# A written four-chunk cycle for the gate stage, rows from chunk 26 on, and a fifth row buffer

## The chip, the core and the metric

The kernel runs on one core of one Trainium2 chip. The metric is the device time of the whole program in microseconds; smaller is better.

## What is computed

The reference is two transformer blocks over 256 tokens of width 1024. Everything that the change touches lies in the last part of the second block, an expert layer (PEER) with 16,384 experts. Cut to that part:

```python
def peer_ffn(h, w_pq, peer_keys, peer_u, peer_v):
    q = (ht @ w_pq).reshape(T, 8, 2, 128)
    sub = jnp.einsum('thpc,hpnc->thpn', q, peer_keys)
    s_top, i_top = lax.top_k(sub, 16)
    ...                                        # 16 best pairs of each head
    best_s, pos = lax.top_k(cand_s, 16)
    expert = jnp.take_along_axis(cand_i, pos, axis=-1)
    gate = jax.nn.softmax(best_s, axis=-1)     # 8 heads x 16 = 128 experts a token
    def chunk(args):
        xc, ec, gc = args
        u = jnp.take(peer_u, ec, axis=0)
        act = jax.nn.gelu(jnp.einsum('cd,ckd->ck', xc, u))
        vv = jnp.take(peer_v, ec, axis=0)
        return jnp.einsum('ck,ckd->cd', gc * act, vv)
```

`peer_u` and `peer_v` are 16,384 x 1024 in float32, 64 MiB each.

## The kernel before

The kernel computes the expert layer in two ways at once. For the last 160 tokens (`N`) it is dense: all experts' scores are computed, multiplied by a gate that is zero for experts not chosen, and the result is summed over all experts. For the first 96 tokens (`TS`) it is sparse: only the chosen experts' rows are fetched.

**The dense part, score stage.** The experts come in 128 chunks of 128. `wget_raw` hands out the next weight tile of 128x1024 float32 (0.524 MB), which SyncE loads ahead (`_dma`) into a ring of 13 buffers (`home`, with `RB` = 3; four more for a time at the start). For each chunk eight products (`u_dot`, L1599; each is two matmul records in the trace, 16 a chunk) write one PSUM bank of a ring of three (`psum`). For chunks 0 to 43 (`u_chunk`, L1609) ScalarE writes the gelu of it into `act`. From chunk `U0` = 44 on (`u_mul`), tokens whose gate is already known get their gelu into a buffer `ut` (L1617; four buffers, `UT`) and VectorE multiplies it into the gate that stands in `act` (L1620); the other tokens' gelu goes straight into `act` (L1619).

**The gates.** `topk` finds the chosen experts of a token as a pair of indices and a gate; `pick` transposes them so that `ib` and `jb` hold the two indices and the gate, in two float16 parts (`gb[0]` high, `gb[1]` low). `g_batch` makes the gates of 8 tokens for all experts: VectorE builds one-hot tiles (`onehots`: `eq` L1543, `jo` L1544, and `io` as `eq` times the high and the low gate, L1546), 16 float16 matmuls (L1555) make a 128x128 gate matrix of each token in PSUM, and that is multiplied into finished chunks of `act` by VectorE (L1564) or copied by ScalarE (L1566) into chunks yet to come. There are 20 batches, spread over chunks 44 to 125.

**The output stage.** Chunk by chunk, eight products of a `peer_v` tile with `act` add up in four PSUM banks (`acc`, L1684).

**The sparse part.** `sparse` is a generator; each step fetches one 128x1024 tile of expert rows (0.524 MB) by an indirect DMA that GpSimd issues (L1503) into one of `SB` = 4 buffers `ug`. The first 96 steps take rows of `peer_u`, and VectorE multiplies them with the tokens' vectors and sums (L1508). Then the next 96 take rows of `peer_v`, and VectorE adds them, weighted, to `sacc` (L1520). At the end TensorE sums `sacc` over pairs (`pair`, L1698), the columns go into `fT` (L1691, L1693, L1702), are transposed back (`back`, L1675), added to `xl` (L1677), normalized and stored. The copies of `acc` into `fT` on VectorE are ordered behind the last row step.

In the program text, rows start at chunk 44: `step()` after every chunk asks for 192 steps in 222 chunks. The program is ordered for each engine by a planner that simulates the time; an instruction that stands later in the text may be drawn forward on its engine where the planner sees it ready. `behind` adds an order between two instructions of one engine for the planner, without a wait on the chip. The loads of GpSimd's queue (`xl`, `slot`, rows) stand in one order, too.

Of the kernel before, what the change touches and what calls it, by code (L numbers as in the profile page):

```python
# [9 lines left out]
F32 = mybir.dt.float32  # L10
F32R = mybir.dt.float32r
BF = mybir.dt.bfloat16
FP16 = mybir.dt.float16
# [8 lines left out]
D = 1024  # L22
# [110 lines left out]
class Kernel:  # L133
# [1240 lines left out]
    def topk(self, R, K, subs):  # L1374
        nc, V, A, G = self.nc, self.nc.vector, self.nc.scalar, self.nc.gpsimd
        iota = R.iota
        self.ib, self.jb, *self.gb = [R.pool.tile([128, 256], FP16, name=n) for n in ("ib", "jb", "g1", "g2")]
        self.iota2 = R.pool.tile([128, 128, 2], FP16, name="iota2")
        V.tensor_copy(self.iota2, iota[:, :, None].to_broadcast([128, 128, 2]))
        it16 = K.tile([128, 16, 16], FP16, name="it16")  # L1380
# [67 lines left out]
    def pick(self, K, tt, prev):  # L1448
        nc, V, A = self.nc, self.nc.vector, self.nc.scalar
        ps = self.bank(self.ptk, "tk")  # L1450
        for i, a in enumerate(self.picked[tt]):
            self.behind(nc.tensor.transpose(ps[:, 128 * i:128 * i + 128], a.rearrange("p h k -> p (h k)"), self.eye),
                        prev)
        t0 = slice(tt * 128, tt * 128 + 128)
        for d, i in ((self.ib, 1), (self.jb, 2)):
            A.activation(d[:, t0], ps[:, 128 * i:128 * i + 128], AF.Copy)
        g = K.tile([128, 128], F32, name="gres", bufs=2)
        V.tensor_scalar(g, ps[:, 0:128], GSCALE, None, op0=OP.mult)
        V.tensor_copy(self.gb[0][:, t0], g)
        V.tensor_tensor(self.gb[1][:, t0], g, self.gb[0][:, t0], OP.subtract)  # L1460


    TG = ((0, 64), (64, 32))
    TS = 96
    SB = 4

    def rows_init(self, SP):
        nc, V = self.nc, self.nc.vector
# [29 lines left out]
    def sparse(self):  # L1498
# [6 lines left out]
        slots = [(g, s) for g, (t0, n) in enumerate(self.TG) for s in range(t0, t0 + n)]  # L1505
        for g, s in slots:
            t = fetch(self.io["u_rows"], s)
            V.scalar_tensor_tensor(t, t, 1.0, self.hrow[g], op0=OP.mult, op1=OP.mult, accum_out=self.sdot[:, s:s + 1])  # L1508
            yield
        A.activation(self.sw, self.sdot, AF.Gelu_apprx_tanh)  # L1510
        V.scalar_tensor_tensor(self.sw, self.sw, GSCALE, self.slot[:, 1], op0=OP.mult, op1=OP.mult)
# [18 lines left out]
    SP = ("VVVVVG", "VVVVVG")  # L1530
    OB = (2, 2)
    U0 = 44
    SC = 222
    U1 = 126
    UT = 4

    def onehots(self, O, t0):
        V = self.nc.vector
        jo, eq = [O.tile([128, 4, 128, 2], FP16, name=n, bufs=b) for n, b in (("jo", self.OB[0]), ("eq", 1))]
        io = O.tile([128, 2, 4, 128, 2], FP16, name="io", bufs=self.OB[1])  # L1540
        bc = lambda a: a[:, t0:t0 + 8].rearrange("p (b t) -> p b t", t=2)[:, :, None, :].to_broadcast([128, 4, 128, 2])
        iob = self.iota2[:, None].to_broadcast([128, 4, 128, 2])
        V.tensor_tensor(eq, iob, bc(self.ib), OP.is_equal)  # L1543
        V.tensor_tensor(jo, iob, bc(self.jb), OP.is_equal)  # L1544
        for q in range(2):
            V.tensor_tensor(io[:, q], eq, bc(self.gb[q]), OP.mult)  # L1546
        return jo, io

    def g_batch(self, O, pg, act, t0, i):
        nc, V, A = self.nc, self.nc.vector, self.nc.scalar  # L1550
        ps = self.bank(pg, "g", 2)
        jo, io = self.onehots(O, t0)
        for t in range(8):
            for q in range(2):
                nc.tensor.matmul(ps[:, t // 4, 128 * (t % 4):128 * (t % 4) + 128], jo[:, t // 2, :, t % 2],  # L1555
                                 io[:, q, t // 2, :, t % 2], start=q == 0, stop=q == 1)
        pv = ps.rearrange("p b (t i) -> p i (b t)", t=4)
        for k in range(2):
            m = self.U0 if k == 0 else 128 - self.U0
            o = self.U0 * k  # L1560
            n = min(max(i - o, 0), m)
            w = act[k][:, :, t0 - self.TS:t0 - self.TS + 8]
            if n:
                V.tensor_tensor(w[:, 0:n], w[:, 0:n], pv[:, o:o + n], OP.mult)  # L1564
            if n < m:
                A.activation(w[:, n:m], pv[:, o + n:o + m], AF.Copy)  # L1566

    def peer(self):
        nc, V, A, G, tc = self.nc, self.nc.vector, self.nc.scalar, self.nc.gpsimd, self.tc
# [17 lines left out]
        with ExitStack() as st:  # L1587
# [18 lines left out]
            def u_chunk(i):  # L1606
                ps = self.psum()
                m = u_dot(ps[:, 0:N])
                A.activation(at(i), ps[:, 0:N], AF.Gelu_apprx_tanh)  # L1609
                return m  # L1610

            def u_mul(i, n, U):
                ps = self.psum()
                u_dot(ps[:, 0:N])
                w = at(i)
                t = U.tile([128, N], F32, name="ut")
                A.activation(t[:, 0:n], ps[:, 0:n], AF.Gelu_apprx_tanh)  # L1617
                if n < N:
                    A.activation(w[:, n:], ps[:, n:N], AF.Gelu_apprx_tanh)  # L1619
                V.tensor_tensor(w[:, 0:n], w[:, 0:n], t[:, 0:n], OP.mult)  # L1620
            with tc.tile_pool(name="route", bufs=1) as K:
                R = type("R", (), dict(iota=iota, pool=PT))
                with self.ps_pool("prt") as self.prt:
                    subs = self.route(R, K, h)
                with self.ps_pool("ptk") as self.ptk:
                    self.topk(R, K, subs)
                    self.depth = 10 + self.RB
                    for i in range(self.U0):
                        m = u_chunk(i)
                        if i == self.U0 - 4:  # L1630
                            for tt in range(2):
                                self.pick(K, tt, m)
# [2 lines left out]
            A1 = st.enter_context(tc.tile_pool(name="act1", bufs=1))  # L1635
            act.append(A1.tile([128, 128 - self.U0, N], F32, name="act1"))
            U = st.enter_context(tc.tile_pool(name="ut", bufs=self.UT))
            sparse, done = self.sparse(), [0, 0]

            def step():  # L1640
                done[0] += 1
                while done[1] * self.SC < done[0] * 2 * TS:
                    next(sparse, None)
                    done[1] += 1
            with tc.tile_pool(name="oh", bufs=2) as O, self.ps_pool("pg", 2) as pg:
                i, nb = self.U0, N // 8
                for b in range(nb):
                    self.g_batch(O, pg, act, TS + 8 * b, i)
                    while i < 128 and (i - self.U0) * nb < (b + 1) * (self.U1 - self.U0):
                        u_mul(i, 8 * b + 8, U)  # L1650
                        step()
                        i += 1
                while i < 128:
                    u_mul(i, N, U)
                    step()
                    i += 1
            pa = st.enter_context(self.ps_pool("pa"))
            acc = [self.bank(pa, f"acc{i}") for i in range(4)]
            x = self.bt.tile([128, 2, 1024], F32, name="xl", tag="bighi")
# [21 lines left out]
            for i in range(128):  # L1681
                w = self.wget_raw()
                for d in range(8):
                    nc.tensor.matmul(part(d), w[:, 128 * d:128 * d + 128], at(i),  # L1684
                                     start=i == 0 and d % 2 == 0, stop=i == 127, skip_group_check=True)
                step()
            for _ in sparse:
                pass
            for d in range(8):
# [80 lines left out]
```

## Time and profile before

| | |
|---|---|
| median of 3 runs | 1314.06 us (1309.58 to 1322.44) |
| profiled execution | 1311.89 us, span 1309.8 us |
| granted TensorE clock, mean | 0.969 |
| TensorE matmul busy | 1238.3 us (95%) |
| VectorE busy | 909.0 us (69%) |
| ScalarE busy | 447.7 us (34%) |
| GpSimd busy | 445.3 us (34%) |
| moved from and to HBM | 356.22 MB read, 2.12 MB written |

Busy time is a share of the whole span; a stage's limit is read from the stage. Of 0.524 MB loads there are 128 of `peer_u`, 128 of `peer_v` and 192 tiles of rows. The score stage runs from 675.6 to 978.7 us, the output stage from 978.9 to 1284.3.

### The profile page before, as it was taken

What the parts mean: (1) busy time and instruction counts of PE and PEld (TensorE: products, weight loads), DVE (VectorE), ACT (ScalarE), POOL (GpSimd) and SP (SyncE); (2) the same over time, 40 slices, a digit from 0 to 9 for tenths busy, and PEclk for the clock granted to TensorE, in tenths of its full rate; (3) what the DMA queues carried; (4) which work ended last, traced back from release to release, by engine and by line L of the source; (5) the groups of instructions that cost most, each with busy time, mean ns of one, the idle gap of its engine ahead of it and who ended that gap; (6) DMA issues with size and microseconds to landing.
All of it is one profiled execution on the core that took longest, in us unless ns stands there. A gap on an engine that the chain in (4) does not pass through costs nothing.

```text
span 1309.8 us, 22554 instructions
## 1 busy us (share of the span) xinstructions
PE 1238.3 (95%) x8649; PEld 1158.9 (88%) x8650; DVE 909.0 (69%) x1810; ACT 447.7 (34%) x895; POOL 445.3 (34%) x400
## 2 busy tenths in 40 slices
PE   6799989999999999998999999999999999999995
PEld 5688869988979997996899999999999999888884
DVE  8996765889668897468789766777764445454455
ACT  5337655666557755645532112221110000000001
POOL 6931021555105755003300432223233333333332
PEclk9978899999999998998999999999999999999996
DMA  6322346889826655346677999999999999999993
GB/s 204 100 87 72 134 164 215 316 301 333 256 91 236 215 168 168 126 143 216 245 273 244 348 409 362 366 360 354 356 378 409 409 409 409 408 409 409 409 405 123
DMA packets 103115, 361.50 MB, mean 276 GB/s; under 512 B 15136, under 2 KB 15328, under 8 KB 102624
## 3 DMA queue, kind: packets, MB, share of 16 engines
q1 hardware_dynamic: 71904, 251.28, 52.7%
q0 software_dynamic: 30816, 108.26, 21.8%
q8 instruction: 68, 1.11, 0.4%
q10 hardware_dynamic: 288, 0.52, 0.1%
q14 instruction: 39, 0.32, 0.1%
HBM read 356.22 MB, written 2.12 MB: 274 GB/s over the span
## 4 chain that ended last, share of the span: by engine, by line
PE 52%; DMA 19%; DVE 15%; issue 6%; POOL 5%; ACT 3%; SPq 0%; DVEq 0%; POOLq 0%; ACTq 0%
PE m L1599 17%; PE m L272 16%; DMA ug<-peer_v,slot 16%; PE acc L858 4%; DVE wlo L231 3%; PE acc L1105 2%; DVE sacc L1520 2%; POOL ug L1503 2%; DMA adaw<-w_ada 2%; PE acc L873 1%; PE g L1555 1%; PE pq L1105 1%; DVE adaacc L407 1%; POOL adaacc L412 1%; DVE work L1337 1%
## 5 line engine op out<-in xcount | busy, mean ns | idle before, releaser
L1684 PE MATMUL acc<-act,raw 128*128 128x160 f32 x2048 | 296.6, 302 | 8.9 <-DMA raw<-peer_v 1.8
L1684 PEld LDWEIGHTS acc<-act,raw 128*128 128x128 f32 x2048 | 280.1, 190 | 25.3 <-DMA raw<-peer_v 22.6
L1599 PE MATMUL m<-hN,raw 128*128 128x160 f32 x2048 | 285.1, 301 | 2.6 <-ACT act L1609 2.6
L1599 PEld LDWEIGHTS m<-hN,raw 128*128 128x128 f32 x2048 | 280.6, 191 | 2.8 <-ACT act L1609 2.8
L231 DVE TENSOR_TENSOR wlo<-raw,whi 128x1024 fp32r<-128x1024 f32 x150 | 229.3, 1539 | 69.7 <-ACT whi L226 68.2
L226 ACT ACTIVATE whi<-raw 128x1024 fp32r<-128x1024 f32 x166 | 173.8, 1055 | 129.6 <-PE m L272 56.9
L1520 DVE SCALAR_TENSOR_TENSOR sacc<-ug,sw,sacc 128x1024 f32<-128x1024 f32 x94 | 120.8, 1285 | 122.1 <-DMA ug<-peer_v,slot 122.0
L1503 POOL DMA_INDIRECT ug<-u_rows,slot x96 | 98.7, 1028 | 212.4 <-DVE ug L1508 124.2
L1508 DVE SCALAR_TENSOR_TENSOR ug<-ug,hrow 128x1024 f32<-128x1024 f32 x96 | 117.2, 1221 | 47.1 <-DMA ug<-u_rows,slot 45.8
L1503 POOL DMA_INDIRECT ug<-peer_v,slot x96 | 91.7, 955 | 159.4 <-DVE sacc L1520 145.1
L272 PE MATMUL m<-h_hi,wlo 128*128 128x256 f32 x768 | 115.9, 291 | 6.8 <-DVE wlo L231 4.9
L272 PE MATMUL m<-h_hi,whi 128*128 128x256 f32 x768 | 116.4, 290 | 2.6 <-ACT h_hi L916 2.6
L272 PE MATMUL m<-h_lo,whi 128*128 128x256 f32 x768 | 115.8, 290 | 2.0 <-DVE h_lo L917 2.0
L272 PEld LDWEIGHTS m<-h_hi,wlo 128*128 128x128 f32 x768 | 103.6, 196 | 9.2 <-DVE wlo L231 5.7
L272 PEld LDWEIGHTS m<-h_hi,whi 128*128 128x128 f32 x768 | 105.2, 196 | 6.9 <-ACT h_hi L916 3.5
L272 PEld LDWEIGHTS m<-h_lo,whi 128*128 128x128 f32 x768 | 104.2, 196 | 3.1 <-DVE h_lo L917 2.4
L1691 ACT ACTIVATE fT<-acc,gt 128x160 f32<-128x160 f32 x4 | 1.3, 393 | 246.9 <-DVE fT L1693 246.9
L410 POOL TENSOR_TENSOR adaacc<-adaacc,adaw 128x1024 f32<-128x1024 f32 x24 | 66.5, 2773 | 48.5 <-ACT adaw L409 45.7
L1617 ACT ACTIVATE ut<-m 128x8 f32<-128x8 f32 (+19 forms) x84 | 20.3, 242 | 126.9 <-PE m L1599 121.3
L231 POOL TENSOR_TENSOR wlo<-raw,whi 128x1024 fp32r<-128x1024 f32 x16 | 40.3, 2525 | 49.7 <-ACT whi L226 43.9
L1620 DVE TENSOR_TENSOR act<-act,ut 128x8 f32<-128x8 f32 (+19 forms) x84 | 20.6, 246 | 49.1 <-ACT ut L1617 45.9
L1609 ACT ACTIVATE act<-m 128x160 f32<-128x160 f32 x44 | 13.1, 304 | 69.6 <-PE m L1599 67.7
(523 smaller groups left out, 1736.1 us busy)
## 6 DMA issues: line engine op xcount, KB each, us to landing
raw<-peer_u SPq DMA_DIRECT2D x128, 512.0 KB
raw<-peer_v SPq DMA_DIRECT2D x128, 512.0 KB
raw<-w_in SPq DMA_DIRECT2D x62, 512.0 KB
adaw<-w_ada SPq DMA_DIRECT2D x48, 512.0 KB
raw<-w_gu SPq DMA_DIRECT2D x44, 512.0 KB
raw<-w_down SPq DMA_DIRECT2D x22, 512.0 KB
raw<-w_out SPq DMA_DIRECT2D x16, 512.0 KB
raw<-w_pq SPq DMA_DIRECT2D x16, 512.0 KB
```

The source lines that it names most:

```text
L226: i = self.nc.scalar.activation(hi, t, AF.Copy)
L231: i = e.tensor_tensor(lo, t, hi.bitcast(F32), OP.subtract)
L272: self.nc.tensor.matmul(out, w(k), x(k), start=start and c == 0, stop=stop and c == last)
L410: G.tensor_tensor(accs[1], accs[1], w, OP.add)
L858: self.nc.tensor.matmul(acc[2 * tt + n], a[:, k, tt * 128:tt * 128 + 128], w[:, 512 * n:512 * n + 512], start=first and (tt, n) not in see ...
L1105: self.nc.tensor.matmul(out, a[:, 2 * c + kk, tt * 128:tt * 128 + 128], w[:, 512 * kk:512 * kk + 512], start=c + i + kk == 0, stop=c == 3 ...
L1503: G.indirect_dma_start(t, None, rows, bass.IndirectOffsetOnAxis(self.slot[:, 0, s:s + 1].bitcast(U32), 0))
L1508: V.scalar_tensor_tensor(t, t, 1.0, self.hrow[g], op0=OP.mult, op1=OP.mult, accum_out=self.sdot[:, s:s + 1])
L1520: self.last = V.scalar_tensor_tensor(self.sacc[g], t, w, self.sacc[g], op0=OP.mult, op1=OP.add)
L1599: m = nc.tensor.matmul(ps, w[:, 128 * k:128 * k + 128], hN[:, k], start=k == 0, stop=k == 7)
L1620: V.tensor_tensor(w[:, 0:n], w[:, 0:n], t[:, 0:n], OP.mult)
L1684: nc.tensor.matmul(part(d), w[:, 128 * d:128 * d + 128], at(i), start=i == 0 and d % 2 == 0, stop=i == 127, skip_group_check=True)
```

## The change

- From chunk 44 on, each instruction of the score stage on VectorE, ScalarE and TensorE is chained behind the one before it on its engine (`chain`, which uses `behind`). `onehots` and `g_batch` become a generator `gate_batch`, one batch to four chunks: `eq` at the first chunk, `jo` at the second, the high part of `io` at the third, the 16 matmuls behind the products of the fourth, and the application at the first chunk of the next batch. The 20 batches span chunks 44 to 123, and their application ends at chunk 124.
- The low part of `io` is made by ScalarE, one copy of 128x128 with a scale for each of the 8 tokens, four at the second and four at the third chunk; the low gate becomes a float32 tile `gl`. `eq` gets two buffers.
- The `ut` multiplication of a chunk (`late`) stands behind the next chunk's gate instruction and row step.
- Row steps stand in the text from chunk 26 (`S0`) on: 15 before chunk 44, then 70 in the 84 chunks 44 to 127 (three of each four chunks, and the first of every third group), then five to each six output chunks.
- `SB` goes from 4 to 5.

```diff
@@ topk, pick @@
-        self.ib, self.jb, *self.gb = [R.pool.tile([128, 256], FP16, name=n) for n in ("ib", "jb", "g1", "g2")]
+        self.ib, self.jb, self.gb = [R.pool.tile([128, 256], FP16, name=n) for n in ("ib", "jb", "g1")]
+        self.gl = R.pool.tile([128, 256], F32, name="g2")
...
-    SB = 4
+    SB = 5
@@ sparse @@
-            V.scalar_tensor_tensor(t, t, 1.0, self.hrow[g], op0=OP.mult, op1=OP.mult, accum_out=self.sdot[:, s:s + 1])
+            i = V.scalar_tensor_tensor(t, t, 1.0, self.hrow[g], op0=OP.mult, op1=OP.mult,
+                                       accum_out=self.sdot[:, s:s + 1])
+            if self.tail is not None:
+                self.chain(i)
             yield
@@ onehots and g_batch become: @@
+    def chain(self, i, on=True):
+        prev = self.tail.get(i.ins.engine)
+        if prev is not None:
+            self.behind(i, prev)
+        self.tail[i.ins.engine] = i
+        return i
+
+    def gate_batch(self, O, pg, act, t0, c):
+        nc, V, A, D = self.nc, self.nc.vector, self.nc.scalar, self.chain
+        jo, eq = [O.tile([128, 4, 128, 2], FP16, name=n, bufs=2) for n in ("jo", "eq")]
+        io = O.tile([128, 2, 4, 128, 2], FP16, name="io", bufs=2)
...
+        def low(ts):
+            for t in ts:
+                D(A.activation(io[:, 1, t // 2, :, t % 2], eq[:, t // 2, :, t % 2], AF.Copy,
+                               scale=self.gl[:, t0 + t:t0 + t + 1]))
+        D(V.tensor_tensor(eq, iob, bc(self.ib), OP.is_equal))
+        yield
+        D(V.tensor_tensor(jo, iob, bc(self.jb), OP.is_equal))
+        low(range(0, 4))
+        yield
+        D(V.tensor_tensor(io[:, 0], eq, bc(self.gb), OP.mult))
+        low(range(4, 8))
+        yield
         ps = self.bank(pg, "g", 2)
+        yield lambda: [D(nc.tensor.matmul(ps[:, t // 4, 128 * (t % 4):128 * (t % 4) + 128], jo[:, t // 2, :, t % 2],
+                                          io[:, q, t // 2, :, t % 2], start=q == 0, stop=q == 1))
+                       for t in range(8) for q in range(2)]
+        i = c()
         pv = ps.rearrange("p b (t i) -> p i (b t)", t=4)
-        for k in range(2):
+        for k in (1, 0):
             m = self.U0 if k == 0 else 128 - self.U0
             o = self.U0 * k
             n = min(max(i - o, 0), m)
             w = act[k][:, :, t0 - self.TS:t0 - self.TS + 8]
+            if n < m:
+                D(A.activation(w[:, n:m], pv[:, o + n:o + m], AF.Copy))
             if n:
-                V.tensor_tensor(w[:, 0:n], w[:, 0:n], pv[:, o:o + n], OP.mult)
-            if n < m:
-                A.activation(w[:, n:m], pv[:, o + n:o + m], AF.Copy)
+                D(V.tensor_tensor(w[:, 0:n], w[:, 0:n], pv[:, o:o + n], OP.mult))
@@ peer @@
...
                     for i in range(self.U0):
                         m = u_chunk(i)
+                        if i >= self.S0 and i % 6:
+                            next(sparse)
...
+                self.tail = {}
+                nb, n, late = N // 8, 0, lambda: None
+                live, cur = None, [0]
+                for i in range(self.U0, 128):
+                    c, cur[0] = i - self.U0, i
+                    mm = None
+                    if c % 4 == 0:
+                        if live is not None:
+                            next(live, None)
+                            n += 8
+                        live = self.gate_batch(O, pg, act, TS + 2 * c, lambda: cur[0]) if 2 * c < N else None
+                    if live is not None:
+                        mm = next(live)
+                    if c % 4 or c % 12 == 0:
+                        next(sparse)
+                    late()
+                    late = u_mul(i, n, U)
+                    if mm is not None:
+                        mm()
+                late()
+                assert n == N and live is None
+                self.tail = None
...
-                step()
+                if i % 6:
+                    next(sparse, None)
```

`u_mul` issues its products, gelus and multiplication through `chain` and returns the multiplication, which the loop above calls as `late`.

## Rows read from the trace of the kernel before

**Rows 1.** Windows, three stages: length, busy us (instructions) of PE, PEld, DVE, ACT, POOL; clock, DMA, GB/s.
```profile
780.00:979.00 199.00, 199.00 (x1640) 198.28 (x1638) 140.84 (x304) 39.13 (x179) 58.59 (x57) 1.00 0.98 363
979.00:1098.00 119.00, 119.00 (x879) 119.00 (x878) 57.86 (x74) 0.59 (x2) 43.17 (x46) 1.00 1.03 409
1098.00:1282.00 184.00, 175.11 (x1158) 158.73 (x1157) 89.40 (x70) 0.00 (x0) 66.85 (x71) 1.00 1.02 406
```

**Rows 2.** The output line: duration min/median/max ns, first and last start, idle time before it.
```profile
L1684 PE MATMUL acc<-act,raw x2048: 299/299/403, 978.9 to 1284.0; 128*128 128x160 f32 x187
...
  DMA raw<-peer_v: 24.4, 66
  issue: 2.5, 7
```

**Rows 3.** DMA queues, 1050 to 1170 us: packets, MB, share (weights q1, rows q0).
```profile
q1 hardware_dynamic: 6785, 24.70, 51.6%
q0 software_dynamic: 6654, 24.22, 50.7%
```

**Rows 4.** Chain of waits, 1050 to 1062 us: start, us, what.
```profile
1050.35 1.30 DVE sacc L1520
...
1051.91 8.60 DMA ug<-peer_v,slot
...
1060.60 1.29 DVE sacc L1520
```

**Rows 5.** Waits of SyncE's queue, 780 to 960 us: total, times, longest.
```profile
SPq L201 <- PE m L1599: 138.3, 69, 2.7
```

**Rows 6.** Waits of GpSimd, 780 to 960 us.
```profile
POOL ug L1503 <- DVE ug L1508: 52.9, 26, 5.3
```

**Rows 7.** Timeline of TensorE at the end, with idle time and releaser.
```profile
1284.14 0.55 PE L1698 MATMUL m<-pair,sacc 128*128 128x64 f32 x4
1290.51 6.18 PE L1698 MATMUL m<-pair,sacc 128*128 128x32 f32 x28 [5.82 <-DVE sacc L1520]
```

**Rows 8.** Chain of waits at the end.
```profile
1289.17 1.30 DVE sacc L1520
...
1300.19 0.69 DVE xl L1677
```

**Rows 9.** Windows around the end; the clock is the third figure from the right.
```profile
1282.00:1284.00 2.00, 2.00 (x15) 2.00 (x16) 1.80 (x2) 0.00 (x0) 0.73 (x2) 1.00 0.69 209
1288.00:1290.00 2.00, 0.00 (x0) 0.00 (x0) 0.83 (x1) 0.00 (x0) 0.00 (x0) 0.50 0.10 39
```

**Rows 10.** Chain of waits in the gate stage, one cycle.
```profile
856.54 0.92 PE g L1555 x16
857.45 8.75 PE m L1599 x64
866.20 0.92 PE g L1555 x16
```

**Rows 11.** Groups of VectorE, 780 to 978 us: busy us, mean ns, idle before.
```profile
L1546 DVE TENSOR_TENSOR io<-eq,g 128x1024 f16<-128x1024 f16 x36 | 23.2, 685 | 0.0
L1543 DVE TENSOR_TENSOR eq<-iota,ib 128x1024 f16<-128x1024 f16 x18 | 12.3, 686 | 0.0
```

**Rows 12.** Timeline: gate applications, a `ut` multiplication, the nearest copy of ScalarE.
```profile
857.71 0.86 DVE L1564 TENSOR_TENSOR act<-act,g 128x352 f32<-128x352 f32 x2 [0.59 <-PE g L1555]
870.47 0.24 DVE L1620 TENSOR_TENSOR act<-act,ut 128x80 f32<-128x80 f32 x1
...
770.30 0.28 ACT L1456 ACTIVATE ib<-tk 128x128 f16<-128x128 f32 x1
```

**Rows 13.** Instructions on tile `ug`: to 767 us, to 978 us, and VectorE's idle time for it to 978.
```profile
L1508 DVE SCALAR_TENSOR_TENSOR ug<-ug,hrow x14: 1210/1225/1226, 730.2 to 764.0; 128x1024 f32<-128x1024 f32 x14
L1508 DVE SCALAR_TENSOR_TENSOR ug<-ug,hrow x71: 1210/1219/1249, 730.2 to 977.5; 128x1024 f32<-128x1024 f32 x71
  DMA ug<-u_rows,slot: 12.8, 9
```

More of the change, by code (lines that the diff above doesn't have):

```diff
@@ L1458, in pick @@
         V.tensor_scalar(g, ps[:, 0:128], GSCALE, None, op0=OP.mult)
-        V.tensor_copy(self.gb[0][:, t0], g)
-        V.tensor_tensor(self.gb[1][:, t0], g, self.gb[0][:, t0], OP.subtract)
+        V.tensor_copy(self.gb[:, t0], g)
+        V.tensor_tensor(self.gl[:, t0], g, self.gb[:, t0], OP.subtract)
     TG = ((0, 64), (64, 32))
     TS = 96
-    SB = 4
+    SB = 5
     def rows_init(self, SP):
@@ L1532 @@
     U0 = 44
-    SC = 222
+    S0 = 26
     U1 = 126
     UT = 4
[L1537 to L1540, printed above, removed]
+    def chain(self, i, on=True):
[4 more added lines that the diff above has]
+        return i
@@ L1541, in onehots @@
+    def gate_batch(self, O, pg, act, t0, c):
+        nc, V, A, D = self.nc, self.nc.vector, self.nc.scalar, self.chain
+        jo, eq = [O.tile([128, 4, 128, 2], FP16, name=n, bufs=2) for n in ("jo", "eq")]
+        io = O.tile([128, 2, 4, 128, 2], FP16, name="io", bufs=2)
         bc = lambda a: a[:, t0:t0 + 8].rearrange("p (b t) -> p b t", t=2)[:, :, None, :].to_broadcast([128, 4, 128, 2])
         iob = self.iota2[:, None].to_broadcast([128, 4, 128, 2])
-        V.tensor_tensor(eq, iob, bc(self.ib), OP.is_equal)
@@ L1544, in onehots @@
[L1544 to L1550, printed above, removed]
-        ps = self.bank(pg, "g", 2)
[L1552 to L1556, printed above, removed]
+        def low(ts):
+            for t in ts:
+                D(A.activation(io[:, 1, t // 2, :, t % 2], eq[:, t // 2, :, t % 2], AF.Copy,
+                               scale=self.gl[:, t0 + t:t0 + t + 1]))
@@ L1612, in u_mul @@
             def u_mul(i, n, U):
-                ps = self.psum()
-                u_dot(ps[:, 0:N])
+                ps, D = self.psum(), self.chain
+                w = self.wget_raw()
+                for k in range(8):
+                    D(nc.tensor.matmul(ps[:, 0:N], w[:, 128 * k:128 * k + 128], hN[:, k], start=k == 0, stop=k == 7))
                 w = at(i)
-                t = U.tile([128, N], F32, name="ut")
-                A.activation(t[:, 0:n], ps[:, 0:n], AF.Gelu_apprx_tanh)
+                t = None
+                if n:
+                    t = U.tile([128, N], F32, name="ut")
+                    D(A.activation(t[:, 0:n], ps[:, 0:n], AF.Gelu_apprx_tanh))
                 if n < N:
-                    A.activation(w[:, n:], ps[:, n:N], AF.Gelu_apprx_tanh)
-                V.tensor_tensor(w[:, 0:n], w[:, 0:n], t[:, 0:n], OP.mult)
+                    D(A.activation(w[:, n:], ps[:, n:N], AF.Gelu_apprx_tanh))
+                return (lambda: D(V.tensor_tensor(w[:, 0:n], w[:, 0:n], t[:, 0:n], OP.mult))) if n else (lambda: None)
+            sparse, self.tail = self.sparse(), None
             with tc.tile_pool(name="route", bufs=1) as K:
@@ L1637, in peer @@
             U = st.enter_context(tc.tile_pool(name="ut", bufs=self.UT))
[L1638 to L1644, printed above, removed]
-            with tc.tile_pool(name="oh", bufs=2) as O, self.ps_pool("pg", 2) as pg:
[L1646 to L1650, printed above, removed]
-                        step()
[L1652 to L1656, printed above, removed]
+            with tc.tile_pool(name="oh", bufs=2) as O, self.ps_pool("pg", 2) as pg:
+                self.tail = {}
[20 more added lines that the diff above has]
+                self.tail = None
             pa = st.enter_context(self.ps_pool("pa"))
@@ L1685, in peer @@
                                      start=i == 0 and d % 2 == 0, stop=i == 127, skip_group_check=True)
-                step()
+                if i % 6:
+                    next(sparse, None)
             for _ in sparse:
```

## The prediction

> **What bounds the kernel now.** I read the page's slices first, then the windows over the last half, then the two queues. From the first score chunk on TensorE is busy nearly without a break, so a time can only be won where it waits. The windows show three stages [rows 1]. In the score stage with gates (780 to 979 us) TensorE is busy 199 of 199 us while the DMA engines move 363 GB/s. In the first part of the output stage (979 to 1098) it is still full, at 409 GB/s. From 1098 to 1282 the DMA still moves 406 GB/s and TensorE is busy 175 of 184 us. 409 GB/s is a ceiling: the stretches from 979 to 1282 us sit at it, whatever was queued. The output line confirms it: between its 2048 matmuls TensorE waited 24.4 us for `raw` and 2.5 us on issue [rows 2].
>
> The queues say who shares that ceiling. While both had work (1050 to 1170) the weights' queue moved 24.70 MB and the row queue 24.22 MB: half each [rows 3]. Rows of 0.524 MB therefore come at 2.56 us each, and the chain shows it: its row steps, four buffers apart, stand at 1050.35 and 1060.60, 10.25 us [rows 4]. In the gate stage it is otherwise: SyncE waits for TensorE to free a weight buffer [rows 5], GpSimd for VectorE to free a row buffer [rows 6]. There the DMA has room, and the rows go only as fast as VectorE gets to them.
>
> At the end the rows are last: the last row step starts at 1289.17, TensorE idles 5.8 us before the bulk of the `pair` matmuls at 1290.51, and they run at half the granted clock [rows 7 to 9].
>
> **The change part by part.** The profiled execution took 1311.9 us for a span of 1309.8, so 2.1 us lie around the span; it is 2.2 us below the median of the three runs shown, 1314.1. I sum against 1311.9.
>
> *TensorE in the gate stage.* The same 84 chunks and 20 gate groups, in the same cycle: 0.92 us of gate matmuls and 8.75 us for four chunks, 9.67 us [rows 10]. Nothing is taken off, so the stage can't get shorter and still ends near 978.7. It gets longer only if an operand is late.
>
> *VectorE in one cycle.* The second gate multiply leaves: 36 `io` instructions at 0.685 us, half of them, 18 in 18 cycles [rows 11]. What stays is `eq`, `jo` (like `eq`) and one `io` at 0.69, two gate applications (0.86 us), four `ut` multiplies at about 0.25 [rows 11, 12], in all 4.0 us. The rows are written in as 3 a cycle and a fourth in every third, 70 in 84 chunks, at 1.22 us [rows 13]: 3.7 us, or 4.9 with the fourth. Sum 7.7 or 8.9 of 9.67 us: it fits, with 0.8 us to spare in the fullest cycle. The gate group of a cycle needs `io` from the third chunk, and TensorE reaches it only after the fourth, so VectorE can be some 2 us late before TensorE sees it. This cover is what hides the whole edit; without it each microsecond costs 20.
>
> *ScalarE* gets the low half of the gates: 8 instructions of 128x128 to f16 a batch. The trace has no such scaled copy; the nearest is the 0.28 us copy into `ib` [rows 12]. Bounds are zero if they all hide, and 8 x 0.28 = 2.2 us a cycle if none does; ScalarE was busy 39 of 199 us in this stage [rows 1], so I take zero. Behind them in its queue stand the gelus that free TensorE's banks; three banks make a delay of two chunks, 4.3 us, harmless.
>
> *Rows from chunk 26 on* is less than it sounds. The planner had already drawn the first rows forward: 14 row steps had begun by 764.0 us [rows 13], well before the first gate matmuls. Now 15 are written there. No term.
>
> *What it does gain* is rows done before the output stage: 71 had begun by 977.5 us [rows 13]; after the change 15 + 70 = 85. I take 13.5 more (71 and a half against 85). They need bandwidth in the gate stage: 84 weights and 70 rows of 0.524 MB in 202 us (84 x 2.19 + 20 x 0.92) are 80.7 MB, 400 GB/s, just below 409. So it holds, but with 2% left, and I expect half a chunk of the weights' lead to be lost.
>
> *Fifth row buffer.* In the output stage the row queue already always had work, since it held its half; five in place of four change nothing there. In the gate stage a buffer is needed again only 12 us after it is freed (5 rows at 2.9 us, less a row step and the issue), against 8.6 us from issue to landing in the full stretch [rows 4]. Zero; between −2 and 0.
>
> *Where the 13.5 rows' time goes.* The row chain ends 13.5 x 2.56 = 34.6 us earlier, 1290.5 to about 1256. TensorE doesn't get that. The weights never had more than half while rows ran, and while the rows run they still take the other half. TensorE's stall of 26.9 us [rows 2] lies in the 184 us from 1098 to 1282: 0.146 us a microsecond. It now stops at 1256: 26 x 0.146 = 3.8 us saved. A chunk is used in (305.6 − 26.9) / 128 = 2.18 us and comes in 2.56, so the lead shrinks by 0.068 chunks a microsecond; half a chunk less brings the first stall forward by 7 us, and 1.0 us back. The last output matmul ends near 1284.3 − 2.8 = 1281.5.
>
> *The end.* Now the output matmuls, not the rows, end last, and the 32 `pair` matmuls follow at once. At the full clock four took 0.55 us (0.137 each), at half 28 took 6.18 (0.22 each) [rows 7, 9]; 32 at 0.137 are 4.4 us. I take the full clock, since it was granted 1.00 until TensorE idled and 0.50 after that [rows 9], and now nothing idles it there. After them the transposes, also at full clock, are hidden in part by VectorE's additions, which then set the pace: I count 8.4 us from the last output matmul to the last addition, where it was 10.4 from 1290.51 to 1300.88 [rows 8], and the 8.9 us behind it unchanged. End 1281.5 + 8.4 + 8.9 = 1298.8; if the clock were half all the same, 1301.5. With 2.1 us around it: **1301 us**, 11 us (0.8%) below the profiled execution. The Trainium skill, *TensorE: Matmul & The Clock Gate*, Part 1, says that the engine's default is the throttled clock and that activity releases it; the rows agree.
>
> The Trainium skill, *DMA: Bandwidth & Descriptors*, section Queues, rings and completion order, says that each DMA engine goes round robin between queues that have work. The halves measured above agree; by a rule of equal turns the first rival below can't come about.
>
> **The rivals.**
> *The shared total decides* (chance 0.12): 13.5 rows are 7.1 MB, 17.3 us at 409 GB/s, and if the weights took what the rows leave, both would end 17.3 us earlier: 1284.3 − 17.3 + 17.3 + 2.1 = 1286. For it: the DMA is full from 979 to 1282. Against it: the equal halves, with 66 waits of TensorE beside them.
> *It doesn't do what it says* (0.18): rows land late or VectorE's written order leaves it waiting for gelus, and fewer than half of the extra rows are done by the output stage. Then only the end gains: 1305 to 1312, say 1308. For it: 2% of bandwidth left. Against it: the landing needs 8.6 us and has 12.
> *The written order holds TensorE* (slower, 0.10): before, VectorE passed over what wasn't ready when the order was planned; now a row that lands late holds, in VectorE's queue, `eq`, `jo`, `io` and the `ut` multiplies, and so the gate matmuls, behind which TensorE's chunks stand. It decides once a cycle's rows are over 2 us late; 1.5 us beyond that costs 20 x 1.5 = 30 us: 1331. Against it: VectorE waited 12.8 us in all, 9 times, for rows before 978 [rows 13].
> *The gate stage is already at its ceiling* (slower, 0.03): if 363 GB/s were all that this stage can move, 400 − 363 = 37 GB/s for 202 us, 7.5 MB or 14 chunks, would be lacking. The lead covers about 8 (0.068 chunks a microsecond from 979 to 1098), 6 chunks at 2.56 us delay the stage by 15, and without a lead the stalls begin 119 us sooner, 17 us: 1333. Against it: 409 GB/s in the very next stage, rows of the same tensor among them. The Trainium skill, *DMA: Bandwidth & Descriptors*, Specifications, gives an HBM limit per core of about 358 GB/s, which would make this the outcome; the trace's 409 contradicts it.
>
> **How the numbers follow.** My forecast, 1301, has 0.57, with 1294 to 1307 from the bounds on the clock at the end, the lead (one chunk is 2 us) and one row either way (0.4 us). 8 in 10 reach from half of the good rival, 1289, to the top of the rival without gain, 1313. About 1% is what a measurement of this kernel can tell from no change; 1% below the median is 1301, below the profiled execution 1299. So the forecast is split: some 0.25 of its 0.57 and the 0.12 of the first rival count as faster, 0.37; the rest of it and the second rival 0.50; slower 0.13.
>
> **What would show it.** Right: TensorE full from 780 to 979 as before at close to 400 GB/s; 84 or 85 row steps by 979; first wait for `raw` around 1090; the row chain ending near 1256, and then 30 us in which TensorE runs without waits and the DMA falls to the weights' 240 GB/s; `pair` matmuls directly behind the output at clock 1.00. Wrong: gaps of TensorE before the gate matmuls; a row lead of only a few; an output stage whose stalls shrink by 17 us rather than 4; or a part before 720 us that the planner orders anew, which nothing in this sum covers.

## The result, and the profile after

The changed kernel takes 1305.58 us in the median of 11 runs (1295.86 to 1310.38), the kernel before, over the same 11 runs, 1316.17 (1309.58 to 1322.44): ratio 0.9912, 95% interval 0.9892 to 0.9932, 10.6 us less. The profiled execution took 1310.38 us (span 1308.6), the slowest of the 11. It began its score stage 11 us later than the profiled execution of the kernel before (686.6 against 675.6), so from here on I compare stages, not ends of spans.

The windows of the changed kernel, one for each stage, with the columns of [rows 1]:

```profile
788.00:990.00 202.00, 202.00 (x1666) 201.24 (x1666) 143.57 (x313) 86.92 (x340) 93.48 (x70) 1.00 1.02 399
990.00:1105.00 115.00, 115.00 (x849) 115.00 (x848) 57.30 (x59) 0.58 (x2) 41.57 (x45) 1.00 1.03 409
1105.00:1262.00 157.00, 148.67 (x979) 134.22 (x978) 77.84 (x61) 0.00 (x0) 54.57 (x58) 1.00 1.03 409
1262.00:1292.50 30.50, 30.50 (x227) 30.50 (x226) 2.44 (x4) 0.90 (x3) 0.00 (x0) 1.00 0.50 200
```

The gate stage is as full as before, with 399 GB/s in place of 363. Then comes the stretch at 409 GB/s with gaps in TensorE, and behind it a stretch that the kernel before doesn't have: 30 us without a gap, at 200 GB/s. That 200 is a mean of two very different parts. With the rows gone the weights alone take the full rate, until nothing is left to load:

```profile
1265.00:1275.00 10.00, 10.00 (x76) 10.00 (x75) 0.00 (x0) 0.00 (x0) 0.00 (x0) 1.00 1.02 406
1278.00:1292.00 14.00, 14.00 (x105) 14.00 (x104) 0.80 (x3) 0.55 (x2) 0.00 (x0) 1.00 0.01 4
```

The row steps on `ug` up to the output stage, and what VectorE waited for there, stand against [rows 13]:

```profile
L1509 DVE SCALAR_TENSOR_TENSOR ug<-ug,hrow x85: 1212/1216/1227, 743.0 to 986.2; 128x1024 f32<-128x1024 f32 x85
...
  DMA ug<-u_rows,slot: 13.9, 10
```

85 row steps in place of 71. The output line, against [rows 2], and the two queues from 1060 to 1180 us, against [rows 3]:

```profile
L1710 PE MATMUL acc<-act,raw x2048: 299/299/403, 989.8 to 1292.2; 128*128 128x160 f32 x187
...
  DMA raw<-peer_v: 24.6, 63
```

```profile
q1 hardware_dynamic: 6752, 24.59, 51.3%
q0 software_dynamic: 6689, 24.35, 51.0%
```

The halves are still there, and so are nearly all of TensorE's waits: 24.6 us where 26.9 stood with its issues. TensorE's first wait in the output stage shows how far ahead the weights' loads are when the stage begins (their lead). The first two groups of its weight loads, in the kernel before and in the changed one (timeline):

```profile
978.72 119.59 PEld L1684 LDWEIGHTS acc<-act,raw 128*128 128x128 f32 x880
1098.54 2.20 PEld L1684 LDWEIGHTS acc<-act,raw 128*128 128x128 f32 x16 [0.23 <-DMA raw<-peer_v]
```

```profile
989.66 119.59 PEld L1710 LDWEIGHTS acc<-act,raw 128*128 128x128 f32 x880
1109.45 2.20 PEld L1710 LDWEIGHTS acc<-act,raw 128*128 128x128 f32 x16 [0.20 <-DMA raw<-peer_v]
```

880 loads, 55 chunks, pass without a wait in both, so the 14 further rows cost the weights none of their lead. At the end the last two row steps of VectorE and TensorE's last groups (timeline: start, us, what, idle time before), against [rows 7]:

```profile
1260.54 1.28 DVE L1524 SCALAR_TENSOR_TENSOR sacc<-ug,sw,sacc 128x1024 f32<-128x1024 f32 x1 [1.29 <-DMA ug<-peer_v,slot]
1263.09 1.28 DVE L1524 SCALAR_TENSOR_TENSOR sacc<-ug,sw,sacc 128x1024 f32<-128x1024 f32 x1 [1.26 <-DMA ug<-peer_v,slot]
```

```profile
1261.78 30.69 PE L1710 MATMUL acc<-act,raw 128*128 128x160 f32 x224
1292.31 3.65 PE L1725 MATMUL m<-pair,sacc 128*128 128x64 f32 x32
```

Rows still come 2.55 us apart, the last one 28 us before the output ends, and the `pair` matmuls follow at once: 32 in 3.65 us.

The stages of all profiled executions, from starts and ends in the traces, in us. Score: first score matmul to first output matmul. Output: from there to the end of the last output matmul. Rows' end: last row step, counted from the first output matmul. Tail: last output matmul to the end of the span. Steps: row steps begun before the output stage.

| | score | output | both | rows' end | tail | steps |
|---|---|---|---|---|---|---|
| before | 303.2 | 305.4 | 608.6 | 311.6 | 25.5 | 71 |
| after | 303.2 | 302.7 | 605.9 | 274.6 | 16.1 | 85 |
| paced | 301.5 | 293.2 | 594.7 | 291.0 | 16.1 | 85 |
| four buffers | 303.3 | 301.8 | 605.1 | 280.6 | 16.1 | 85 |
| 57 steps | 301.5 | 308.6 | 610.1 | 307.9 | 16.1 | 72 |
| 81 steps | 305.5 | 309.6 | 615.1 | 254.3 | 16.1 | 95 |
| before, paced | 303.2 | 297.9 | 601.1 | 314.8 | 36.2 | 71 |
| before, 21 extra matmuls | 301.5 | 307.6 | 609.1 | 310.7 | 22.3 | 71 |
| before, 12 extra matmuls | 303.2 | 305.6 | 608.8 | 311.3 | 24.8 | 71 |
| low half on VectorE | 301.5 | 303.1 | 604.6 | 276.8 | 16.1 | 85 |
| paced, 81 steps | 304.3 | 299.3 | 603.6 | 270.0 | 16.1 | 95 |
| paced, 81 steps, even | 304.4 | 288.4 | 592.8 | 284.8 | 16.1 | 95 |

Between the first two lines 2.7 us went from the output stage and 9.4 from the tail. Apart from the runs with 81 steps, the score stage is 301.5 or 303.2, for a reason that stands in the last section, and what it gains so the output stage can lose again (608.6 against 609.1 for two executions of the same stages); "both" is therefore the figure to compare.

### The profile page after: what moved, and what is told of

Its sections match the earlier page's. It is cut to its first block, busy times and chain, and to the rows that moved or that the text cites. A ratio compares the mean times of both kernels' runs of the same rounds, so it can differ in the third digit from the quotient of the medians.

```text
span 1308.6 us, 22647 instructions
## 1 busy us (share of the span) xinstructions
PE 1236.8 (95%) x8650; PEld 1156.7 (88%) x8650; DVE 896.3 (68%) x1787; ACT 494.9 (38%) x1053; POOL 464.0 (35%) x400
## 4 chain that ended last, share of the span: by engine, by line
PE 51%; DMA 22%; DVE 17%; issue 4%; ACT 2%; POOL 2%; SPq 0%; DVEq 0%; POOLq 0%; ACTq 0%
DMA raw<-peer_v 17%; PE m L1631 14%; PE m L272 13%; PE acc L1710 6%; PE m L1614 4%; PE acc L858 4%; DVE wlo L231 4%; PE acc L1105 3%; DMA adaw<-w_ada 2%; PE acc L873 1%; PE g L1568 1%; POOL adaacc L410 1%; DVE adaacc L407 1%; POOL adaacc L412 1%; DMA bias<-bias 1%
## 5 line engine op out<-in xcount | busy, mean ns | idle before, releaser
L231 DVE TENSOR_TENSOR wlo<-raw,whi 128x1024 fp32r<-128x1024 f32 x150 | 232.0, 1558 | 63.8 <-ACT whi L226 60.9
L1504 POOL DMA_INDIRECT ug<-u_rows,slot x96 | 120.7, 1258 | 149.6 <-DVE act L1639 97.1
L1509 DVE SCALAR_TENSOR_TENSOR ug<-ug,hrow 128x1024 f32<-128x1024 f32 x96 | 116.9, 1218 | 26.9 <-DMA ug<-u_rows,slot 26.9
L272 PE MATMUL m<-h_hi,wlo 128*128 128x256 f32 x768 | 113.0, 286 | 5.4 <-DVE wlo L231 4.8
```

The source lines that it names most:

```text
L231: i = e.tensor_tensor(lo, t, hi.bitcast(F32), OP.subtract)
L272: self.nc.tensor.matmul(out, w(k), x(k), start=start and c == 0, stop=stop and c == last)
L1504: G.indirect_dma_start(t, None, rows, bass.IndirectOffsetOnAxis(self.slot[:, 0, s:s + 1].bitcast(U32), 0))
L1509: i = V.scalar_tensor_tensor(t, t, 1.0, self.hrow[g], op0=OP.mult, op1=OP.mult, accum_out=self.sdot[:, s:s + 1])
```

## The experiments

My theory: while rows run, weights and rows get half of the 409 GB/s each, so the lead of the rows frees bandwidth only where the rows have ended, and most of the gain lies in the tail. Rivals: the shared total decides; the written order or ScalarE's part is what gains; the fifth buffer does. Ratios are to the kernel before, executed beside each run.

**Pacing the rows of the changed kernel.** In the output stage the fetch of a row tile also waits for the last product of the chunk six before the place where its step stands.

```diff
@@ sparse @@
+            if self.pace is not None:
+                self.tc.add_manual_dep(i.ins, self.pace.ins.name, ...)
@@ output stage, at the end of chunk i @@
+                ends.append(m)
+                self.pace = ends[i - self.LAG] if i >= self.LAG else None
                 if i % 6:
                     next(sparse, None)
```

> The changed kernel, and in the output stage each row fetch also waits for the output products of the chunk six before (at most five rows to six chunks). If the two queues share the DMA in halves (my theory), the changed kernel wastes bandwidth after its last row, 30.7 us at 200 GB/s; rows spread over the stage should let it stay near 409 GB/s to the end, the last output matmul coming 291 to 295 us after the first instead of 302.6, and the total 8 to 12 us (0.6 to 0.9%) below the changed kernel: ratio to the kernel before near 0.983. If TensorE's waits in the output stage come from something else than the rows' share (latency of the loads, the weights' queue itself), the output stage stays at 302 us or grows, because rows now end last.

Ratio 0.9832 (0.9794 to 0.9869), median 1294.46 us. The queues from 1060 to 1180, the waits of GpSimd from 1100 to 1262 (total, times, longest), the windows to the end of the output stage, and the output line's wait:

```profile
q1 hardware_dynamic: 7211, 26.27, 54.9%
q0 software_dynamic: 6214, 22.62, 47.3%
```

```profile
POOL ug L1505 <- PE acc L1714: 88.2, 45, 4.2
```

```profile
1100.00:1262.00 162.00, 157.67 (x1091) 148.99 (x1090) 73.06 (x58) 0.00 (x0) 59.70 (x57) 1.00 1.03 409
1262.00:1271.00 9.00, 9.00 (x68) 9.00 (x68) 4.72 (x6) 0.66 (x2) 0.00 (x0) 1.00 0.37 149
```

```profile
  DMA raw<-peer_v: 13.7, 37
```

GpSimd now waits for TensorE, the weights have more than half of the same 409 GB/s, and TensorE's waits fall from 24.6 to 13.7 us. What was won is the bandwidth that lay idle at the end: 30.5 us at 200 GB/s in the changed kernel leave 6.4 MB of 409 GB/s unused, 15.6 us of transfers; here 9 us at 149 leave 2.3 MB, 5.7 us. The difference, 9.9 us, is close to the output stage's 9.5.

**Four row buffers** in the changed kernel, nothing else:

```diff
-    SB = 5
+    SB = 4
```

> The changed kernel with four row buffers instead of five. Theory: the fifth buffer does nothing in the output stage, where the row queue has work all the time, and next to nothing in the gate stage; 85 rows stay 85 and the total stays within 2 us of the changed kernel (ratio to the kernel before 0.990 to 0.993). Rival: the fifth buffer is what lets VectorE find its rows in time; then VectorE waits for rows in the gate stage, fewer than 80 rows are done at its end, and the time goes back by 3 us or more.

Ratio 0.9903 (0.9868 to 0.9938); 85 steps and 605.1 us in both stages. The fifth buffer does nothing that can be measured.

**Fewer and more row steps in the gate stage**, 57 and 81 in place of 70:

```diff
-                    if c % 4 or c % 12 == 0:
+                    if c % 4 in (1, 2) or c % 8 == 3 or c % 24 == 7:
```

> The changed kernel with 57 rows instead of 70 written into the gate stage, so 72 rows are done at its end, as in the kernel before; the written cycle stays. Theory: the row lead is the whole gain, so row chain and end return to those of the kernel before: rows last, TensorE idle at the end, ratio 0.997 to 1.003. Rival: the written order itself gains, and the time stays near the changed kernel's 0.991.

```diff
-                    if c % 4 or c % 12 == 0:
+                    if c % 4 or c % 28 != 24:
```

> The changed kernel with 81 rows in the gate stage, 96 done at its end. Demand there is 165 tiles of 0.524 MB in 202 us, 428 GB/s, over the ceiling of 409. Theory: TensorE still takes its 202 us, living on its lead in weights, of which some 7 chunks are used up (19 GB/s short for 202 us); the output stage then waits from its start on at 0.146 us a microsecond for about 245 us until the rows end: 278 + 36 = 314 us instead of 302.6, total 10 us above the changed kernel (ratio 0.997 to 1.002). Rival, that the total of bytes decides: eleven more rows early are eleven fewer late, and the time stays or falls.

57 steps: ratio 0.9923 (0.9897 to 0.9949), not the 1.0 that I expected. The timeline of TensorE shows why:

```profile
1284.73 6.95 PE L1710 MATMUL acc<-act,raw 128*128 128x160 f32 x45
1291.52 3.65 PE L1725 MATMUL m<-pair,sacc 128*128 128x64 f32 x32
```

Its rows end 0.7 us ahead of the last output matmul, and that is enough for the whole gain of the tail (16.1 us in place of 25.5). I had put that gain down to the lead of 14 rows; it needs only that the rows aren't last. The 13 further rows are worth 610.1 − 605.2 (the mean of after, four buffers and low half on VectorE) = 4.9 us in the two stages.

81 steps: 0.9964 (0.9941 to 0.9987), slower than 70 and just under the expected 0.997 to 1.002. Windows of its gate stage, the first part of its output stage and the end of it, TensorE's waits in the gate stage (total, times, longest), and its weight loads at the start of the output stage:

```profile
788.00:985.00 197.00, 195.40 (x1613) 193.99 (x1612) 154.36 (x325) 82.71 (x329) 87.12 (x77) 1.00 1.03 408
985.00:1100.00 115.00, 111.49 (x783) 106.57 (x782) 55.71 (x51) 0.59 (x2) 40.48 (x43) 1.00 1.03 407
1240.00:1295.00 55.00, 55.00 (x407) 55.00 (x407) 1.00 (x4) 0.61 (x2) 0.00 (x0) 1.00 0.52 194
```

```profile
PE g L1568 <- DVE io L1564: 1.6, 4, 0.4
```

```profile
985.71 63.19 PEld L1710 LDWEIGHTS acc<-act,raw 128*128 128x128 f32 x464
```

The gate stage is at the ceiling. Rows land late there: VectorE waits 43.5 us for them up to 985 where it waited 13.9, and by the written order `io` and the gate matmuls are late with them. TensorE's waits in this stage are for `io`, none is for a weight. In the output stage its first wait for a weight comes after 63 us in place of 120, which is 3.8 chunks of lead (56 us x 0.068), not the 7 that I expected, and afterwards 55 us pass at 194 GB/s. So the two stages came to 615.1 us, the 10 more that I had worked out, but 2 of them in the score stage, where I had put none. More lead of the rows here means less of the weights.

**Pacing the kernel before.** The same edit, without the rest of the change (so with four row buffers).

> The kernel before with the pacing alone: in the output stage a fetch of rows waits for the output products of the chunk six before. Equal halves (my theory): pacing hands the weights bandwidth that is only worth something if the rows have finished early; here 121 row tiles are still to come at the output stage, row traffic runs to its very end anyway, and the total of weights and rows (249 tiles of 0.524 MB, 131 MB, 319 us at 409 GB/s) doesn't fit into less. So the stall of TensorE may shrink, but the rows end as late or later than in the kernel before: ratio 0.998 to 1.005, the last row step still behind the last output matmul. Rival (the pacing itself brings the 1.7% of the paced version over the kernel before, whatever the row lead): ratio 0.985 to 0.992.

Ratio 1.0026 (0.9999 to 1.0053): no gain. TensorE's end, and the output line's wait:

```profile
1283.21 0.55 PE L1704 MATMUL m<-pair,sacc 128*128 128x64 f32 x4
1300.26 6.18 PE L1704 MATMUL m<-pair,sacc 128*128 128x32 f32 x28 [16.50 <-DVE sacc L1524]
```

```profile
  DMA raw<-peer_v: 17.0, 50
```

The output stage is 7.5 us shorter, as in the theory, and TensorE then idles 16.5 us for the rows in place of 5.8. So pacing pays 11 us behind the change and nothing ahead of it. I take the 14 steps of lead to be what is spent on it; no run has the changed kernel's order with pacing and without the lead, so that part is argued.

**The clock at the end.** The kernel before with unused matmuls into a spare bank behind the last output matmul; nothing of the result depends on them. Each of the two versions was executed once, so only stretches inside them are compared.

```diff
+            idle = self.psum()
+            for k in range(21):
+                self.behind(nc.tensor.matmul(idle[:, 0:N], w[:, 0:128], at(127), start=True, stop=True), m)
```

> The kernel before with 21 extra matmuls into a scratch bank, ordered behind the last output matmul; their result is unused. They fill the time in which TensorE idles for the last rows. Theory: the clock falls because TensorE idles, so it now stays at 1.00 and the bulk of the pair matmuls, 28 in 6.18 us before, take about 3.8; the time from the last row step's end to the end of the span shrinks from 19.3 by 2 to 3 us, and the rest of the tail's gain (about 6) is the wait for rows itself. Rival (the clock at the end has another cause, the pair matmuls' own shape for one): 28 still take about 6.2 us.

> The kernel before with 12 extra matmuls behind the output in place of 21. With 21 the clock stayed at 1.00 and the pair matmuls took 3.65 us for 32, but the extra ones overran the last row step by 2.4 us. 12 take about 3.4 us. Theory: the clock holds, or idles into its lower level only for the rest of the wait, and the pair matmuls start within 0.3 us of the last row step's end; if it holds, the stretch from there to the end of the span is 16.3 to 17 us in place of 19.3. Rival (the clock's fall costs the end nothing, other work sets its pace): 19 us.

With 21 (timeline of TensorE, and the clock in the window of its `pair` matmuls):

```profile
1286.29 5.87 PE L1689 MATMUL m<-act,raw 128*128 128x160 f32 x42
1291.99 3.65 PE L1701 MATMUL m<-pair,sacc 128*128 128x64 f32 x32
```

```profile
1292.00:1295.60 3.60, 3.60 (x35) 3.60 (x34) 0.99 (x4) 0.00 (x0) 0.00 (x0) 1.00 0.00 0
```

With 12:

```profile
1284.93 3.42 PE L1689 MATMUL m<-act,raw 128*128 128x160 f32 x24
1288.19 0.55 PE L1701 MATMUL m<-pair,sacc 128*128 128x64 f32 x4
1290.86 5.98 PE L1701 MATMUL m<-pair,sacc 128*128 128x32 f32 x28 [2.12 <-DVE sacc L1520]
```

21 without a gap keep the clock at 1.00, and from the start of `pair` to the end of the span pass 16.7 us (1291.99 to 1308.7), where 19.3 did before: 2.6 us. They also overran the last row step by 2.4 us, so from that step to the end it is 19.1 as before, and my 2 to 3 us didn't show in the span. With 12 TensorE idled 2.1 us, and in the window from 1294 to 1297, over the last of its `pair` matmuls, the granted clock was the low level:

```profile
1294.00:1297.00 3.00, 3.00 (x16) 3.00 (x16) 1.00 (x5) 0.00 (x0) 0.00 (x0) 0.50 0.00 0
```

From the start of the 28 to the end of the span 19.0 us pass, so nothing is won. Of the tail's 9.4 us some 6 to 7 are the wait for the last rows and 2.6 the clock.

**The low half of the gates back on VectorE**, in the changed kernel:

```diff
-        def low(ts):
-            for t in ts:
-                D(A.activation(io[:, 1, t // 2, :, t % 2], eq[:, t // 2, :, t % 2], AF.Copy, ...
-        low(range(0, 4))
...
-        low(range(4, 8))
+        D(V.tensor_tensor(io[:, 1], eq, bc(self.gl), OP.mult))
```

> The changed kernel with the low half of the gates back on VectorE, one instruction of 0.69 us a cycle more there, and none of it on ScalarE. Theory (slack covers either): VectorE then has 8.4 us in a cycle of 9.67 and 9.6 in every third, TensorE's gate matmuls are late by little or nothing, and the time stays within 3 us of the changed kernel's: ratio 0.989 to 0.994. Rival (VectorE's place in the cycle decides, and the move to ScalarE is what makes the written cycle fit): the fullest cycles overrun, some 0.5 to 1 us in each of seven, and with the late gate matmuls behind them 5 to 20 us: ratio 0.996 to 1.006.

Ratio 0.9906 (0.9871 to 0.9941), the same as the changed kernel. Windows from 790 to 985, first the changed kernel, then this one:

```profile
790.00:985.00 195.00, 195.00 (x1615) 194.24 (x1614) 139.31 (x305) 86.01 (x337) 89.30 (x67) 1.00 1.02 400
```

```profile
790.00:985.00 195.00, 195.00 (x1606) 194.28 (x1605) 153.80 (x330) 37.62 (x176) 89.84 (x68) 1.00 1.02 398
```

VectorE is busy 14.5 us more, ScalarE 48 less, TensorE full in both. The move to ScalarE is worth nothing that can be measured by itself.

**Pacing with 81 steps**, first with five steps to each six output chunks as before, then with three to each four, so that the 96 steps left last through the stage:

```diff
-                if i % 6:
+                if i % 4:
```

> The paced version with 81 row steps in place of 70 written into the gate stage. Theory (the shared total decides once the rows are paced): the total of bytes is the same, and the gate stage already moves 400 of 409 GB/s, so at most 202 us x 9 GB/s = 1.8 MB, 4 us, can be won in the gate stage's bandwidth, less about 2 us for the waits of TensorE that 81 steps brought there without pacing: the time within 4 us of the paced version's, ratio 0.981 to 0.987. Rival (weights' lead is what counts and extra rows cost it, paced or not): 5 to 9 us slower than the paced version, ratio 0.987 to 0.991.

> As the paced version with 81 row steps in the gate stage, but with three row steps to each four output chunks in place of five to each six, so that the 96 remaining fetches last through the whole output stage. Theory (once paced, the shared total decides, as long as the rows end with the output matmuls): in the last run of 81 steps the rows ended some 29 us ahead of the output matmuls and left bandwidth unused there (23 us at 78 GB/s, about 7 MB, 18 us at 409 GB/s, of which the weights alone could have used half or less); spread evenly, the row chain ends within 6 us of the last output matmul, and score and output stage together, 603.6 us there, come to 595 to 598: ratio 0.982 to 0.987. Rival (the weights' lead lost in the gate stage is what cost it, and can't be won back): they stay at 600 us or more, ratio 0.988 to 0.993.

The first: 0.9917 (0.9894 to 0.9940), far above what my theory gave and just above the rival's range. The second: 0.9819 (0.9767 to 0.9871), median 1291.92 us, at the lower end of what was expected, and 592.8 us in the two stages, below the 595 to 598. The windows at the ends of their output stages, and for the second one the output line's wait:

```profile
1262.00:1285.00 23.00, 23.00 (x174) 23.00 (x172) 1.54 (x4) 1.55 (x4) 0.00 (x0) 1.00 0.20 78
```

```profile
1262.00:1272.00 10.00, 10.00 (x77) 9.97 (x76) 4.75 (x7) 1.46 (x4) 0.00 (x0) 1.00 0.27 106
```

```profile
  DMA raw<-peer_v: 9.1, 24
```

With the same lead of rows the two differ by 10.8 us in the two stages together. What I had left out was the rate: 96 steps at five to six chunks end some 29 us early, and bandwidth lies idle again. So the lead that the weights lost in the gate stage isn't what cost the first one its time. Spread evenly, 95 steps come to 592.8 us against 594.7 for 85: the intervals of the two paced versions overlap, and a gain of the further ten can't be told from none. Both beat the kernel before and the change.

## Why the prediction was right

**Gate stage unchanged.** Right: 303.2 us in both, TensorE 202.00 of 202. The rows brought it to 399 GB/s; 400 were worked out.

**VectorE fits.** Right. The busy times of its groups in the window of 195 us sum to 161 us, 8.0 a cycle (7.7 or 8.9 predicted), in 139 us of busy time, since the records overlap. That the cover is real is shown by the run with 0.69 us a cycle more.

**ScalarE free.** Right in the term, low in the price. The copies:

```profile
L1557 ACT ACTIVATE io<-eq,g 128x128 f16<-128x128 f16 x160 | 52.3, 435 | 0.0
```

52.3 us in 20 cycles are 2.6 a cycle, above my upper bound of 2.2, all hidden.

**85 rows, row chain 34.6 us earlier.** 85, and 37.0. **Fifth buffer zero.** Shown by the run with four.

**Output stage −2.8.** Measured −2.7; −3.6 if the three like executions of after are set against the three of the kernel before whose output stage is untouched (605.2 against 608.8 in score and output stage together). That −2.7 meets −2.8 so closely is luck, since one of its two terms was wrong. The rows' term, 0.146 us saved in each microsecond without rows, holds: from the 57 steps to the 70 the rows' end moves by 30.6 us (307.9 to 277.3, the mean of the three), which gives 4.5 us, and 4.9 were measured. The lead's term, 1.0 us back for half a chunk lost, does not: the first wait was forecast near 1090, 111 us into the stage, and came at 1109.45, 119.8 us into it, as far as in the kernel before. The gate stage moved its 400 GB/s without using up any lead. Without that term the sum says −3.8, near the −3.6. Why the run with 57 steps, one more than the kernel before had, is 1 to 1.5 us longer in both stages stays open.

**The end.** 16.1 us for 17.3 predicted: the last addition ended 7.4 us after the last output matmul (8.4), the rest took 8.7 (8.9). The 32 `pair` matmuls took 3.65 us where 4.4 were worked out from a group of four. Clock 1.00, as chosen, and with the two runs of extra matmuls its price is shown. One sign was wrong: the DMA didn't fall to the weights' 240 GB/s after the last row, it stayed at 406 until the last weights had landed and then stopped (4 GB/s).

**The sum.** 1301 was forecast and 1305.58 measured. The difference is the base: I summed against one execution of 1311.9 us, 4.3 below the median of the 11 runs (1316.17). The change itself was put at 10.9 us and is 10.6 in the medians. In the stages of the two profiled executions it is 12.1 (2.7 and 9.4) for 11.0 worked out.

What the sum couldn't cover, the part before 720 us, cost the profiled execution of the changed kernel 11 us. The executions of the changed kernel and its variants begin their score stages from 676.6 to 688.6 us, those of the kernel before and its variants from 675.6 to 682.2: the two ranges overlap. The traces show that a new order isn't behind most of the 11 us. VectorE's addition `x` (L1010) starts at 615.26 in the kernel before and at 625.22 in the changed one, so 10.0 of the 11 us are there already, and up to it TensorE, VectorE, ScalarE and GpSimd run the same instructions in the same order in both. What differs up to there is the clock (third figure from the right):

```profile
0.00:615.26 615.26, 573.49 (x3755) 515.79 (x3756) 474.75 (x769) 349.98 (x581) 236.05 (x182) 0.96 0.55 186
0.00:625.22 625.22, 577.75 (x3756) 517.60 (x3756) 477.30 (x770) 349.83 (x581) 234.77 (x182) 0.94 0.55 183
```

By the clock records of the two traces, TensorE stood at the lower level (0.50) for 52 us of the one stretch and 72 of the other. 20 us more at half the clock are 10 us of work, an estimate that is the size of the delay. Whether the lower clock caused it or went along with it is not shown.

**The rivals.** "The shared total decides", 1286, didn't happen: while rows ran, the bytes stood at half each; it is what the paced versions come near to (1294 and 1292). The rival without gain, the written order that holds TensorE, and the ceiling of 363 GB/s are refuted by 85 steps, no gap in the gate stage, and 399 GB/s there. The second of them has a true core, though: with 81 steps late rows do reach TensorE through the written order (four waits for `io`).

## What to carry to other kernels

In this kernel two queues that both had work moved half of the bytes each (24.59 and 24.35 MB). Work that was brought forward in one of them reached the other only after it had run dry, and part of what it freed lay idle at the end. So where two queues share DMA engines that are full, read their bytes over the same stretch, and look for an idle end. If both are there, try giving the queue that isn't urgent a pace, so that both end together, and set the rate anew whenever the amount left changes. Bringing work forward paid in two ways here: a few steps of it took a late engine off the end (9.4 us), and the 13 steps beyond were worth 5 us by themselves; with the rest of the rows paced, some 11 us more were won.

## What had not been expected of the hardware

A wait of TensorE for ScalarE, ahead of the gate stage, is the same in all twelve profiled executions (2.56 to 2.62 us), and what follows isn't. The kernel before, and the paced one (timeline of TensorE, and the window from 725 to 730):

```profile
726.64 18.65 PE L1599 MATMUL m<-hN,raw 128*128 128x160 f32 x123 [2.57 <-ACT act L1609]
```

```profile
725.00:730.00 5.00, 3.36 (x13) 3.36 (x14) 5.00 (x13) 1.97 (x4) 1.79 (x2) 0.68 0.96 312
```

```profile
727.58 17.65 PE L1618 MATMUL m<-hN,raw 128*128 128x160 f32 x128 [2.57 <-ACT act L1628]
```

```profile
725.00:730.00 5.00, 2.43 (x19) 2.42 (x19) 4.97 (x19) 2.29 (x5) 4.09 (x4) 1.00 0.86 274
```

In eight executions the granted clock is 0.66 in the 5 us from the first matmul after the wait, a mean of the lower level (0.50, 1.2 GHz) and the full one (1.00, 2.4 GHz); in four (paced, 57 steps, low half on VectorE, 21 extra matmuls) it stays at 1.00. At 0.66 of the clock 5 us lose 1.7 us, the whole difference between 303.2 and 301.5. At the end an idle stretch of 2.1 us was followed by the low level. So after one and the same wait of 2.6 us either level followed here, and differences of 1.7 us between single executions of this kernel mean nothing.
